# Two hybrid layers on one core: S5 by blocks of four tokens, its rotations and scan on VectorE

## The chip, the cores and the metric

The kernel runs on 1 core of one Trainium2 chip. The metric is device time in microseconds (us) of one launch; 3 runs of the kernel before are at hand, and one execution of it was taken by the hardware profiler. All rows below come from that execution. Engines are PE (TensorE matmul), DVE (VectorE), ACT (ScalarE), POOL (GpSimd) and SP (SyncE, which issues most DMAs).

## What is computed

256 tokens of width 2048 pass through two layers. In each, a norm and one product with `w_in` feed three mixers side by side: NSA (sparse attention, 8 heads), S5 (a diagonal complex state space, width 512) and GDN (gated delta rule, 8 heads of 128). Their outputs go through `w_out` into the residual; an FFN of inner width 5504 with a convolution over three tokens follows. The mixer that the change touches is, cut to what matters:

```python
def s5_mixer(u, lam_re, lam_im, log_dt, b_re, b_im, c_re, c_im, d_skip, w_glu):
    ug = u.reshape(B_, L, 32, 16)                    # 32 groups of 16 channels
    dt = exp(log_dt); mag = exp(lam_re * dt)         # 64 states in a group
    lb_re, lb_im = mag * cos(lam_im * dt), mag * sin(lam_im * dt)
    bb = coef(lb, lam) * (b_re + i b_im)             # complex, [g, p, h]
    bu = einsum('blgh,gph->blgp', ug, bb)            # complex
    x_t = lb * x_(t-1) + bu_t                        # over all 256 tokens
    y = einsum('blgp,ghp->blgh', xr, c_re) - einsum('blgp,ghp->blgh', xi, c_im)
    y = gelu(y + d_skip * ug);  return y * sigmoid(y @ w_glu)
```

Two groups of 16 channels share one tile of 128 states: a *pair*. There are 16 pairs, four of them to each of the four tiles `ct` of 128 channels.

## The kernel before

**Weights.** All large products have the tokens along 256 columns. Weights come from DRAM in tiles of 128x1024 (`raw`, three buffers, issued on SP's queue at L336). ACT rounds each to its high part `whi`, DVE subtracts to get the low part `wlo` (L325 and L326, three buffers each), and every product is three single-pass matmuls: xh·whi, xl·whi, xh·wlo, into the PSUM tile `gps`. A tile of 1024 columns so gives 24 matmuls of 256 columns. `z`, GDN's gate, is computed with tokens on partitions and 512 columns (`gps<-wlo,xh`).

**Order.** `PLANS` gives the emission order of a layer: `xs` (small columns), `u0` to `u3` (S5's input), `tab` (S5's tables), then between `S(` and `S)` the heads `h0` to `h6` of GDN with its solves `g` and gates `z`, while `tick()` hands out S5's queued steps between them; then NSA and the out-projection's passes. The FFN follows in two halves of its 43 tiles f. The scheduler of the framework places the instructions on the engines' queues from there; each engine works its own queue in order.

**GDN head.** `gdn_head` (L1184) squares and sums q and k, takes a power of their norms on POOL (`gsk`, L1213), scales `vt` to `vb` on ACT and builds two triangular matrices, which `gdn_solve` inverts with round trips through DRAM (`scr`, L1258).

**S5.** `s5_tables` (L956) computes in float the coefficients (DVE, 16 columns), the input matrices (six POOL products at L1008 to L1013, eight transposes on PE at L1018, split, written to `parts` in DRAM), and e^{i theta t} for t < 128 as the table `tb`, by doubling (L1043 to L1050, on POOL). Layer 0 runs it after `u0`, layer 1 between the halves of the FFN of layer 0. Then each pair (`s5_pair`, L1070) reads `ub` from `parts` (L1078), makes two matmuls of 256 columns, rotates by `tb` from PSUM (L1087, L1088, DVE), adds and subtracts on POOL (L1089, L1090), scans the decay over 4 pieces of 128 (L1097, DVE, two pieces for the real and two for the imaginary part, with a small turn by `pend` between, L1102, L1103), rotates back on POOL (L1107 to L1110), and `s5_out` (L1113) multiplies by C: eight matmuls per tile that each fill 32 of 128 rows (`mpsm<-tX,cm`). POOL makes what `either()` (L494) doesn't give to DVE; here numbers 0 and 4 alone go to DVE, so all of S5's numbers, 8 to 14, go to POOL.

## Time and profile before

| what | value |
|---|---|
| three runs, us | 2607.79, 2611.43 (median), 2614.37 |
| span of the profiled execution, us | 2613.3 |
| PE, DVE, ACT, POOL busy | 96%, 72%, 46%, 19% |
| mean granted TensorE clock | 0.978 |
| read from HBM over the span | 172 GB/s |

No time is given for the profiled execution apart from its span, first to last instruction, so 2613.3 is taken as its own time; it lies between the runs. Busy time is the sum of an engine's instruction records; matmuls are pipelined, so PE's records overlap one another, and a share near 100% says only that PE is seldom empty. A clock of 1.00 is 2.4 GHz. The stages by time are: to 334 us S5 and GDN of layer 0 (from 28 us on), to 548 NSA and out-projection, to 1328 the FFN (with the tables of layer 1 at 830 to 877), to 1377 the start of layer 1, to 1631 its S5 and GDN, to 1882 its NSA and out-projection, to 2610 its FFN.

### The profile page before, as it was taken

What the parts mean: (1) busy time and instruction counts of PE and PEld (TensorE: products, weight loads), DVE (VectorE), ACT (ScalarE), POOL (GpSimd) and SP (SyncE); (2) the same over time, 40 slices, a digit from 0 to 9 for tenths busy, and PEclk for the clock granted to TensorE, in tenths of its full rate; (3) what the DMA queues carried; (4) which work ended last, traced back from release to release, by engine and by line L of the source; (5) the groups of instructions that cost most, each with busy time, mean ns of one, the idle gap of its engine ahead of it and who ended that gap; (6) DMA issues with size and microseconds to landing.
All of it is one profiled execution on the core that took longest, in us unless ns stands there. A gap on an engine that the chain in (4) does not pass through costs nothing.

```text
span 2613.3 us, 51295 instructions
## 1 busy us (share of the span) xinstructions
PE 2519.4 (96%) x20686; PEld 2426.6 (93%) x20686; DVE 1884.8 (72%) x3252; ACT 1203.4 (46%) x1883; POOL 493.1 (19%) x530
## 2 busy tenths in 40 slices
...
GB/s 276 178 166 124 124 184 155 95 210 169 180 184 197 182 186 183 182 185 190 199 210 176 164 133 120 215 128 99 188 180 185 185 179 181 189 182 182 184 192 166
DMA packets 170974, 456.72 MB, mean 175 GB/s; under 512 B 25040, under 2 KB 55152, under 8 KB 170736
## 3 DMA queue, kind: packets, MB, share of 16 engines
...
q0 software_dynamic: 512, 0.98, 0.1%
...
HBM read 434.81 MB, written 15.48 MB: 172 GB/s over the span
## 4 chain that ended last, share of the span: by engine, by line
PE 74%; DVE 13%; POOL 5%; DMA 4%; issue 3%; ACT 1%; SPq 0%; DVEq 0%; ACTq 0%; POOLq 0%
PE gps L293 69%; DVE wlo L326 4%; DVE tW L1097 2%; DVE cva L441 2%; PE mpsh L293 2%; PE mpss L293 2%; PE mpsm L293 1%; DMA raw<-w 1%; POOL bt L1255 1%; POOL tX L1107 1%; POOL ub L1257 1%; ACT whi L325 1%; POOL s5tmp L1108 1%; POOL s5tmp L1089 1%; DMA ks<-ks 1%
## 5 line engine op out<-in xcount | busy, mean ns | idle before, releaser
L325 ACT ACTIVATE whi<-raw 128x1024 fp32r<-128x1024 f32 (+5 forms) x824 | 824.8, 1002 | 1070.9 <-PE gps L293 717.8
L326 DVE TENSOR_TENSOR wlo<-raw,whi 128x1024 fp32r<-128x1024 f32 (+5 forms) x824 | 985.0, 1196 | 454.2 <-ACT whi L325 450.8
L293 PE MATMUL gps<-xh,wlo 128*128 128x256 f32 x3904 | 1121.4, 287 | 15.7 <-DVE wlo L326 15.6
L293 PE MATMUL gps<-xh,whi 128*128 128x256 f32 x3904 | 1120.1, 287 | 8.9 <-DVE cvp L434 6.2
L293 PE MATMUL gps<-xl,whi 128*128 128x256 f32 x3904 | 1118.1, 287 | 0.0
L293 PEld LDWEIGHTS gps<-xh,wlo 128*128 128x128 f32 x3904 | 759.9, 195 | 22.4 <-DVE wlo L326 18.0
L293 PEld LDWEIGHTS gps<-xh,whi 128*128 128x128 f32 x3904 | 760.2, 195 | 15.4 <-DVE cvp L434 7.2
L293 PEld LDWEIGHTS gps<-xl,whi 128*128 128x128 f32 x3904 | 760.0, 195 | 2.0 <-issue 1.4
L293 PE MATMUL gps<-gh,wlo 128*128 128x256 f32 x1376 | 390.2, 284 | 4.5 <-DVE wlo L326 4.4
L293 PE MATMUL gps<-gl,whi 128*128 128x256 f32 x1376 | 389.9, 283 | 0.0
L293 PE MATMUL gps<-gh,whi 128*128 128x256 f32 x1376 | 389.5, 283 | 0.0
L293 PEld LDWEIGHTS gps<-gh,wlo 128*128 128x128 f32 x1376 | 264.4, 192 | 5.3 <-DVE wlo L326 5.3
L293 PEld LDWEIGHTS gps<-gl,whi 128*128 128x128 f32 x1376 | 264.4, 192 | 0.0
L293 PEld LDWEIGHTS gps<-gh,whi 128*128 128x128 f32 x1376 | 264.2, 192 | 0.0
L434 DVE TENSOR_TENSOR cvp<-gps,R 128x256 f32<-128x256 f32 x220 | 92.6, 422 | 83.4 <-PE gps L293 83.4
L293 PE MATMUL gps<-mh,wlo 128*128 128x256 f32 x512 | 150.4, 297 | 1.0 <-DVE wlo L326 1.0
L293 PE MATMUL gps<-mh,whi 128*128 128x256 f32 x512 | 150.4, 296 | 0.8 <-ACT whi L325 0.7
L293 PE MATMUL gps<-ml,whi 128*128 128x256 f32 x512 | 150.7, 296 | 0.0
L293 PEld LDWEIGHTS gps<-mh,wlo 128*128 128x128 f32 x512 | 102.4, 201 | 2.4 <-DVE wlo L326 1.2
L293 PEld LDWEIGHTS gps<-mh,whi 128*128 128x128 f32 x512 | 102.2, 201 | 1.4 <-ACT whi L325 1.2
L293 PEld LDWEIGHTS gps<-ml,whi 128*128 128x128 f32 x512 | 102.5, 201 | 0.6 <-issue 0.4
L441 DVE SCALAR_TENSOR_TENSOR cva<-cvp,parm,cva 128x255 f32<-128x255 f32 x144 | 95.6, 664 | 0.9
...
## 6 DMA issues: line engine op xcount, KB each, us to landing
...
raw<-w SPq DMA_DIRECT2D x192, 448.0 KB
...
```

Of the source, the lines that this page charges most:

```text
L293: self.nc.tensor.matmul(out, lhsT, rhs, start=start, stop=stop)
L325: self.nc.scalar.activation(out=hi, in_=src, func=AF.Copy)
L326: (engine or self.nc.vector).tensor_tensor(lo, src, hi.bitcast(F32), OP.subtract)
L434: nc.vector.tensor_tensor(p, ps, R, OP.mult)
L441: nc.vector.scalar_tensor_tensor(a[:, j:], p[:, :T - j], tap(n - 1 - j), a[:, j:], OP.mult, OP.add)
L1089: self.either(10).tensor_tensor(A[:, 0:256], A[:, 0:256], B[:, 256:512], OP.add)
L1097: nc.vector.tensor_tensor_scan(W[:, o:o + SCAN], mg, A[:, o:o + SCAN], ini[j], OP.mult, OP.add)
L1107: nc.gpsimd.tensor_tensor(v(X), v(W), cb, OP.mult)
L1108: nc.gpsimd.tensor_tensor(v(B), v(W), sb, OP.mult)
L1255: be.tensor_tensor(t[:, 0:n, 0:m], ub[:, 0:n, j:j + 1].to_broadcast([4 * nb, n, m]), bk[:, j:j + 1, n:].to_broadcast([4 * nb, n, m]), OP.mult)
L1257: be.tensor_tensor(ub[:, 0:n, n:], ub[:, 0:n, n:], t[:, 0:n, 0:m], OP.subtract)
```

## The change

A block of four tokens is one step. The input of a step is now the four tokens' channels along 128 partitions (`U`, read back from `us` in DRAM, four reads of 32 partitions per tile), so per pair one full-precision matmul of 64 columns for each of the real and imaginary parts. One scan of 512 elements covers four pairs, two parts and 64 steps (the decay `m4` is set to 0 at the start of each 64). Both rotations and their sums go to DVE. The output of token j in a block takes three products per pair: from the block's own inputs (a triangular matrix of 96 rows), from the real and from the imaginary state before it.

These need new matrices per layer: for each `ct` `s5_blocks` multiplies the input coefficients and C by powers of lambda (by recurrence, `times`), transposes two of the results, multiplies C and B for the triangular one, and writes 640 columns per pair to `parts`. The emission order gets `t0` to `t3` among the `u`s of layer 0; for layer 1 the blocks come in the second half of the FFN of layer 0, ahead of f = 24, 28, 32 and 36. The table `tb` ends at 64 columns. `either(12)` is POOL. The old functions stand above; of the diff, new functions and the call sites:

```diff
-     ("xs u0 tab u1 u2 u3 S( h0 h1 h2 z0 h3 g0 h4 g2 h5 z1 h6 S) N( kc vc q0 ks g4 h7 cmp q1 kw q2 key P5 "
+     ("xs u0 tab u1 t0 u2 t1 u3 t2 t3 S( h0 h1 h2 z0 h3 g0 h4 g2 h5 z1 h6 S) N( kc vc q0 ks g4 h7 cmp q1 kw q2 key P5 "
       "P0 q3 res att g6 p0 a0 a1 o0 p1 N) o1 p2 o2",
       ((13, 11, 8, 4, 5, 12, 6), (10, 15, 14, 9), (7, 0, 1, 2, 3)), 0.8869, (0, 4)),
...
-SCAN = 128
-NS = T // SCAN
+SUB = 4
+TABLES = (24, 28, 32, 36)
+NC4 = T // SUB
...
                 for f in fs:
+                    if hf and not last and f in TABLES:
+                        self.l += 1
+                        self.s5_blocks(TABLES.index(f))
+                        self.l -= 1
...
                 elif k < 8:
-                    self.split_to(mh[k], ml[k], self.so[:, k - 4, :])
+                    blk = lambda v: v.rearrange("p (c r) -> p c r", r=SUB)
+                    self.split_to(blk(mh[k]), blk(ml[k]), self.so[:, k - 4, :].rearrange("p (r c) -> p c r", r=SUB))
...
                 u = self.uT[int(d)]
-                nc.vector.tensor_tensor(u, ps, self.R, OP.mult)
-                hl = [self.slot("uh", F32R), self.slot("ul", F32R)]
-                self.split_to(*hl, u)
-                for i in range(2):
-                    nc.sync.dma_start(self.parts[self.l][i::2, int(d), :, 0:256].rearrange("r c t -> c r t"),
-                                      hl[i].bitcast(F32).rearrange("p (o t) -> p o t", o=1).to_broadcast([128, 2, T]))
+                blk = lambda v: v.rearrange("p (c r) -> p c r", r=SUB)
+                nc.vector.tensor_tensor(u.rearrange("p (r c) -> p c r", r=SUB), blk(ps), blk(self.R), OP.mult)
+                nc.sync.dma_start(self.us[self.l][int(d)], u)
...
+            elif a == "t":
+                if self.l == 0:
+                    self.s5_blocks(int(d))
...
+        self.lam, self.coef = [], []
+        for to, by, nm in ((self.lam, (br, bi), "l"), (self.coef, (cr, ci), "c")):
+            for i, v in enumerate(by):
+                w = s5.tile([128, 16, 2], F32, name=f"s5{nm}{i}")
+                nc.vector.tensor_copy(w, v.rearrange("p (q o) -> p q o", o=1).to_broadcast([128, 16, 2]))
...
+        self.m4 = st("m4")
+        tt(self.m4, mag, mag, OP.mult)
+        tt(self.m4, self.m4, self.m4, OP.mult)
+        pc, pq = square(*square(cs, sn))
+        self.tb = tb = s5.tile([128, 2, 16, NC4], F32, name="tb")
+        self.s5v = self.pool("s5v", 1, "right")
...
+        gt = self.either(12).tensor_tensor
+        while n < NC4:
...
+    def s5_blocks(self, ct):
+
+        nc, s5 = self.nc, self.s5v[1]
+        gt = self.either(12).tensor_tensor
+        src = self.ap[f"s5m{self.l}"].rearrange("p m (t q h) -> p m t q h", t=4, q=4)[:, :, ct]
+
+        V = s5.tile([128, 4 * 512], F32, name="s5V", tag="s5V")
+        v6 = V.rearrange("p (q r b s h) -> p q r b s h", q=4, r=2, b=2, s=4)
+        at = lambda m: bass.AP(tensor=V.tensor, offset=V.offset + 32 * (3 - m),
+                               ap=[V.ap[0], [256, 8], [128 + 32 * (2 * m - 3), 2], [1, 32]])
+        sb = s5.tile([128, 4, 2, 32], F32, name="s5b", tag="s5b")
+        for r in range(2):
+            nc.scalar.dma_start(sb[:, :, r, :], src[:, r])
+            nc.scalar.dma_start(v6[:, :, r, 1, 0, :], src[:, 2 + r])
+
+        def times(out, x, by, n):
+
+            shape = [128, 8, n, 32]
+            t = [self.s5t()[:, 0:256 * n].rearrange("p (a b h) -> p a b h", a=8, b=n) for _ in range(2)]
+            for i in range(2):
+                w = by[i][:, 4 * ct:4 * ct + 4].rearrange("p q (r a b) -> p (q r) a b", a=1, b=1)
+                gt(t[i], x, w.to_broadcast(shape), OP.mult)
+            gt(out[:, 0::2], t[0][:, 0::2], t[1][:, 1::2], OP.subtract)
+            gt(out[:, 1::2], t[0][:, 1::2], t[1][:, 0::2], OP.add)
+
+        times(at(0)[:, :, 0:1], sb.rearrange("p q (r a) h -> p (q r) a h", a=1), self.coef, 1)
+        nb = s5.tile([128, 4, 32], F32, name="s5n", tag="s5n")
+        self.either(12).tensor_scalar(nb, v6[:, :, 1, 0, 3, :], -1.0, None, OP.mult)
+        for m in range(3):
+            times(at(m + 1), at(m), self.lam, 2)
+
+        d = self.parts[self.l][4 * ct:4 * ct + 4]
...
+        for r in range(2):
+            nc.sync.dma_start(rows(384 + 128 * r, 128), v6[:, :, r, 1].rearrange("p q s h -> p q (s h)"))
+            pt = self.mps("s")
+            for q in range(4):
+                nc.tensor.transpose(pt[:, 128 * q:128 * q + 128], v6[:, q, r, 0].rearrange("p s h -> p (s h)"),
+                                    self.c("ident"))
+            g = s5.tile([128, 512], F32, name="s5g", tag="s5g")
+            nc.scalar.activation(out=g, in_=pt, func=AF.Copy)
+            nc.sync.dma_start(rows(128 * r, 128), g.rearrange("p (q s) -> p q s", q=4))
+
+        W = s5.tile([128, 4, 4, 32], F32, name="s5W", tag="s5W")
+        self.either(12).memset(W, 0.0)
+        pt = self.mps("s")
+        p4 = pt.rearrange("p (q j h) -> p q j h", q=4, j=4)
+        for q in range(4):
+            for r in range(2):
+                for i in range(3):
+                    self.mm(p4[32 * i:32 * i + 32, q, i + 1:4, :].rearrange("p j h -> p (j h)"),
+                            nb[:, q, :] if r else v6[:, q, 0, 0, 3, :],
+                            v6[:, q, r, 1, 0:3 - i, :].rearrange("p j h -> p (j h)"), start=(r == 0), stop=(r == 1))
+        for i in range(3):
+            o = slice(32 * i, 32 * i + 32)
+            nc.scalar.activation(out=W[o, :, i + 1:4, :], in_=p4[o, :, i + 1:4, :], func=AF.Copy)
+        nc.sync.dma_start(rows(256, 128), W.rearrange("p q j h -> p q (j h)"))
+        if ct == 3:
+            self.close(self.s5v[0])
...
+        st = {}
+        self.later(lambda: self.s5_in(ct, st), lambda: self.s5_scan(ct, st), lambda: self.s5_out(ct, st))
+
+    def s5_in(self, ct, st):
+        nc, s5 = self.nc, self.s5
+        U = s5.tile([128, 4, NC4 + 2], F32, name="s5U", tag="s5U", bufs=2)
+        ends = bass.AP(tensor=U.tensor, offset=U.offset, ap=[U.ap[0], [NC4 + 2, 4], [NC4, 2]])
+        nc.gpsimd.memset(ends, 0.0)
+        d = self.us[self.l]
+        for i in range(4):
+            o = 0 if i == 3 else 1
+            nc.sync.dma_start(U[32 * i:32 * i + 32, :, o:o + NC4],
+                              d[ct, :, NC4 * ((i + 1) % 4):NC4 * ((i + 1) % 4) + NC4].rearrange("(q h) c -> h q c", q=4))
+        st["U"], st["g"] = U, []
+        bu = self.mps()
         for q in range(4):
-            self.later(lambda q=q: xs.__setitem__(q, self.s5_pair(ct, q)))
-        self.later(lambda: self.s5_out(ct, xs))
-
-    def s5_pair(self, ct, q):
+            g = s5.tile([128, 256], F32, name="s5gi", tag="s5gi", bufs=4)
+            nc.sync.dma_start(g, self.parts[self.l][4 * ct + q, :, 0:256])
+            for r in range(2):
+                o = 128 * q + 64 * r
+                self.mm(bu[:, o:o + 64], g[:, 128 * r:128 * r + 128], U[:, q, 0:NC4])
+        sh = [128, 4, 2, NC4]
+        v = lambda t: t.rearrange("p (q r c) -> p q r c", q=4, r=2)
+        tb = lambda i: self.tb[:, i, 4 * ct:4 * ct + 4].rearrange("p q (r c) -> p q r c", r=1).to_broadcast(sh)
+        A, B = self.s5t(), self.s5t()
+        tt = nc.vector.tensor_tensor
+        tt(v(A), v(bu), tb(0), OP.mult)
+        tt(v(B), v(bu), tb(1), OP.mult)
+        tt(v(A)[:, :, 0], v(A)[:, :, 0], v(B)[:, :, 1], OP.add)
+        tt(v(A)[:, :, 1], v(A)[:, :, 1], v(B)[:, :, 0], OP.subtract)
+        m = s5.tile([128, 512], F32, name="s5m", tag="s5m", bufs=2)
+        m4 = self.m4[:, 4 * ct:4 * ct + 4].rearrange("p (q r c) -> p q r c", r=1, c=1)
+        nc.gpsimd.tensor_copy(v(m), m4.to_broadcast(sh))
+        nc.gpsimd.memset(v(m)[:, :, :, 0:1], 0.0)
+        st["A"], st["m"], st["tb"], st["v"] = A, m, tb, v
+        for q in range(4):
+            g = s5.tile([128, 384], F32, name="s5go", tag="s5go", bufs=5)
+            nc.sync.dma_start(g, self.parts[self.l][4 * ct + q, :, 256:640])
+            st["g"].append(g)
+
+    def s5_scan(self, ct, st):
         nc, s5 = self.nc, self.s5
-        sh = [128, 2, NS, SCAN]
...
+        tt, v, tb = nc.vector.tensor_tensor, st["v"], st["tb"]
...
+        nc.vector.tensor_tensor_scan(W, st["m"], st["A"], 0.0, OP.mult, OP.add)
+        X = s5.tile([128, 512], F32, name="tX", tag="tX", bufs=4)
         B = self.s5t()
...
+        tt(v(X), v(W), tb(0), OP.mult)
+        tt(v(B), v(W), tb(1), OP.mult)
+        tt(v(X)[:, :, 0], v(X)[:, :, 0], v(B)[:, :, 1], OP.subtract)
+
+        nc.vector.scalar_tensor_tensor(v(X)[:, :, 1], v(X)[:, :, 1], -1.0, v(B)[:, :, 0], OP.mult, OP.subtract)
+        st["X"] = X
...
+        U, X, g = st["U"], st["v"](st["X"]), st["g"]
+        for j in range(SUB):
+            for i in range(3):
+                for q in range(4):
+                    w = g[q][:, 128 * i + 32 * j:128 * i + 32 * j + 32]
+                    self.mm(yp[32 * q:32 * q + 32, 64 * j:64 * j + 64], w[0:96] if i == 0 else w,
+                            U[0:96, q, 1:NC4 + 1] if i == 0 else X[:, q, i - 1], start=(i == 0), stop=(i == 2))
```

`order` of the instructions on an engine's queue follows at three places, engine, line, operation, and what is written and read. On POOL, layer 0, around the power `gsk` of the second head, L1213 before and L1270 after. Before, tables (L1045, L1050), then pairs:

```order
L1213 TENSOR_TENSOR gsk<-gS,cst 128x2
L1045 TENSOR_TENSOR tb<-tb,s5tmp 128x8x64
L1050 TENSOR_TENSOR tb<-tb,s5tmp 128x8x64
L1089 TENSOR_TENSOR s5tmp<-s5tmp 128x256
L1090 TENSOR_TENSOR s5tmp<-s5tmp 128x256
L1107 TENSOR_TENSOR tX<-tW,tb 128x512
L1108 TENSOR_TENSOR s5tmp<-tW,tb 128x512
L1089 TENSOR_TENSOR s5tmp<-s5tmp 128x256
L1090 TENSOR_TENSOR s5tmp<-s5tmp 128x256
L1109 TENSOR_TENSOR tX<-tX,s5tmp 128x256
L1110 TENSOR_TENSOR tX<-tX,s5tmp 128x256
```

and after, where `times` is L1073 to L1075, `s5l` are the powers' lambda and `s5c` the input's coefficients:

```order
L1073 TENSOR_TENSOR s5tmp<-s5V,s5l_529 128x512
L1073 TENSOR_TENSOR s5tmp<-s5V,s5l_531 128x512
L1074 TENSOR_TENSOR s5V<-s5tmp 128x4x2x32
L1075 TENSOR_TENSOR s5V<-s5tmp 128x4x2x32
L1073 TENSOR_TENSOR s5tmp<-s5V,s5l_529 128x512
L1073 TENSOR_TENSOR s5tmp<-s5V,s5l_531 128x512
L1073 TENSOR_TENSOR s5tmp<-s5b,s5c_533 128x256
L1073 TENSOR_TENSOR s5tmp<-s5b,s5c_535 128x256
L1270 TENSOR_TENSOR gsk<-gS,cst 128x2
L1074 TENSOR_TENSOR s5V<-s5tmp 128x4x2x32
L1075 TENSOR_TENSOR s5V<-s5tmp 128x4x2x32
```

The power stood between parts of two S5 pairs; it now stands between the products of the second block and those of the third (the 256-column products start a block).

On SP, layer 0, at the first reads of S5's inputs. Before, with `ub` as the input of a pair:

```order
L336 DMA raw<-w 128x1024
L1023 DMA parts_88<-s5tmp 128x4x128 x2
L336 DMA raw<-w 128x1024 x2
L1078 DMA ub<-parts_88 128x1x512 x2
L336 DMA raw<-w 128x1024
L1078 DMA ub<-parts_88 128x1x512
L336 DMA raw<-w 128x1024 x2
L1078 DMA ub<-parts_88 128x1x512
L336 DMA raw<-w 128x1024 x2
```

and after, where `s5gi` and `s5go` are the matrices of one pair for input and output, and `s5U` the inputs of a tile:

```order
L337 DMA raw<-w 128x1024
L1093 DMA parts_90<-s5g 128x4x128
L1108 DMA parts_90<-s5W 128x4x128
L1130 DMA s5gi<-parts_90 128x256
L1124 DMA s5U<-us_88 32x4x64 x4
L1130 DMA s5gi<-parts_90 128x256 x3
L1150 DMA s5go<-parts_90 128x384 x4
L1124 DMA s5U<-us_88 32x4x64 x4
L1130 DMA s5gi<-parts_90 128x256 x4
L1150 DMA s5go<-parts_90 128x384
L1303 DMA scr_86<-nq 128x2x128
L337 DMA raw<-w 128x1024 x2
```

Before, loads of weights (`raw`) stood between the single reads; now the reads of the first two tiles stand in a row behind the fourth block's writes (L1093, L1108).

On PE, layer 0, at the first input products of S5. Before, behind the products of k and q of GDN's first head:

```order
L293 MATMUL gps<-xl,whi 128x256
L293 MATMUL mpsh<-gk 128x256
L293 MATMUL mpsh<-gk 128x128
L293 MATMUL mpsh<-gq,gk 128x256
L293 MATMUL mpsh<-gq,gk 128x128
L293 MATMUL mpsm<-ub 128x256 x2
L293 MATMUL gps<-xh,wlo 128x256
```

and after, where `mpss<-gU,gP` is GDN's solve of the first two heads:

```order
L294 MATMUL gps<-xh,wlo 128x256
L294 MATMUL mpss<-gU,gP 32x32 x3
L294 MATMUL mpsm<-s5U,s5gi 128x64 x2
L1282 MATMUL mpsh<-cst,vt 128x128
L294 MATMUL mpsm<-s5U,s5gi 128x64 x4
L1282 MATMUL mpsh<-cst,vt 128x128
L294 MATMUL mpss<-gU,gP 32x32 x2
L294 MATMUL mpsm<-s5U,s5gi 128x64 x2
L294 MATMUL mpss<-gU,gP 32x32 x11
```

The first input products moved from the first head's products to the first solve, from behind 455 `gps` products to behind 1017 (counted from the start of the program).

## Rows read from the trace of the kernel before

**Rows 1.** The page: busy time, share of the span and instructions of each engine.

```profile
PE 2519.4 (96%) x20686; PEld 2426.6 (93%) x20686; DVE 1884.8 (72%) x3252; ACT 1203.4 (46%) x1883; POOL 493.1 (19%) x530
```

**Rows 2.** Windows: stretch, busy us (instructions) of PE, PEld, DVE, ACT, POOL; clock, DMA.

```profile
28.00:334.00 306.00, 272.30 (x2132) 244.22 (x2132) 279.90 (x561) 118.50 (x202) 199.28 (x194) 0.94 0.51 160
830.00:877.00 47.00, 42.54 (x349) 41.73 (x348) 38.99 (x52) 16.73 (x18) 41.03 (x46) 1.00 0.65 195
1377.00:1631.00 254.00, 229.57 (x1856) 207.39 (x1855) 237.47 (x449) 101.47 (x179) 142.86 (x137) 0.95 0.45 144
1882.00:2610.00 728.00, 727.51 (x6048) 727.31 (x6048) 464.47 (x636) 336.16 (x432) 0.00 (x0) 1.00 0.56 182
```

**Rows 3.** Groups on PE, 1377 to 1631 us: busy us, mean ns | idle before.

```profile
L293 PE MATMUL gps<-xh,wlo 128*128 128x256 f32 x321 | 95.9, 299 | 5.2 <-DVE wlo L326 5.2
...
L293 PE MATMUL gps<-wlo,xh 128*128 128x512 f32 x64 | 25.6, 400 | 1.4 <-DVE wlo L326 1.3
...
L293 PE MATMUL mpsh<-cst,gsq 128*128 128x1 f32 x56 | 7.9, 259 | 4.1 <-ACT gsq L1205 4.1
...
L293 PE MATMUL mpsm<-tX,cm 128*32 128x256 f32 x64 | 6.6, 390 | 1.2 <-POOL tX L1109 1.0 <-POOL tX L1110 0.2
...
L293 PE MATMUL mpss<-gU,gP 64*64 64x64 f32 x16 | 1.3, 224 | 0.0
```

**Rows 4.** Timeline of PE from 138 us: start, duration.

```profile
138.91 0.40 PE L293 MATMUL gps<-wlo,xh 128*128 128x512 f32 x1
139.14 0.40 PE L293 MATMUL gps<-whi,xl 128*128 128x512 f32 x1
```

**Rows 5.** Groups on DVE, 1377 to 1631 us.

```profile
L326 DVE TENSOR_TENSOR wlo<-raw,whi 128x1024 fp32r<-128x1024 f32 x58 | 81.0, 1396 | 4.8 <-ACT whi L325 4.7
L1097 DVE TENSOR_TENSOR_SCAN tW<-s5mag,s5tmp 128x128 f32<-128x128 f32 x32 | 21.1, 673 | 7.0 <-POOL s5tmp L1089 7.0
...
L1097 DVE TENSOR_TENSOR_SCAN tW<-s5mag,s5d,s5tmp 128x128 f32<-128x128 f32 x32 | 13.6, 466 | 0.1
...
L1087 DVE TENSOR_TENSOR s5tmp<-mpsm,tb 128x512 f32<-128x512 f32 x16 | 10.8, 677 | 0.3 <-PE mpsm L293 0.3
...
L434 DVE TENSOR_TENSOR cvp<-gps,R 128x256 f32<-128x256 f32 x20 | 8.2, 409 | 0.1
L1195 DVE TENSOR_TENSOR_SCAN E<-eb,cst 128x256 f32<-128x256 f32 x7 | 5.9, 838 | 0.0
...
L1103 DVE TENSOR_TENSOR s5d<-s5e 128x2 f32<-128x2 f32 x16 | 2.5, 157 | 0.1
```

**Rows 6.** Groups on DVE, 1900 to 2100 us, in the FFN of layer 1.

```profile
L326 DVE TENSOR_TENSOR wlo<-raw,whi 128x1024 fp32r<-128x1024 f32 x70 | 85.8, 1226 | 38.1 <-ACT whi L325 38.1
L434 DVE TENSOR_TENSOR cvp<-gps,R 128x256 f32<-128x256 f32 x35 | 14.9, 425 | 17.3 <-PE gps L293 17.3
```

**Rows 7.** Groups on POOL, 1377 to 1631 us.

```profile
L1108 POOL TENSOR_TENSOR s5tmp<-tW,tb 128x512 f32<-128x512 f32 x16 | 31.2, 1951 | 0.0
...
L1109 POOL TENSOR_TENSOR tX<-tX,s5tmp 128x256 f32<-128x256 f32 x16 | 13.4, 836 | 0.7
```

**Rows 8.** Groups on PE, 28 to 334 us.

```profile
L1018 PE MATMUL mpsm<-cst,s5tmp 128*128 128x128 f32 x8 | 1.2, 276 | 0.1
```

**Rows 9.** Groups on POOL, 830 to 877 us.

```profile
L1045 POOL TENSOR_TENSOR tb<-tb,s5tmp 128x512 f32<-128x512 f32 x3 | 5.8, 1927 | 0.0
...
L1043 POOL TENSOR_TENSOR tb<-tb,s5pc 128x512 f32<-128x512 f32 x3 | 3.1, 1048 | 0.0
```

**Rows 10.** Timeline of POOL: start, duration.

```profile
46.37 1.05 POOL L1009 TENSOR_TENSOR s5tmp<-s5tmp,s5ci 128x512 f32<-128x512 f32 x1 [1.73 <-DVE s5t L1052]
...
122.26 1.02 POOL L1213 TENSOR_TENSOR gsk<-gS,cst 128x2 f32<-128x2 f32 x1 [0.80 <-DVE fe L1212]
```

**Rows 11.** Instructions of tile `ub`: ns (min, median, max), first and last start.

```profile
L1078 SPq DMA_DIRECT2D ub<-parts x32: 524/535/743, 73.5 to 1559.9; - x32
```

**Rows 12.** Groups on DVE, 830 to 877 us.

```profile
L326 DVE TENSOR_TENSOR wlo<-raw,whi 128x1024 fp32r<-128x1024 f32 x6 | 9.7, 1623 | 2.3 <-ACT whi L325 2.3
```

128 lines of the change are left out of this document (27 added, 101 removed), and 2 rows, old and new, of the table PLANS.

## Prediction, made before the changed kernel was run

> **What bounds the kernel now.** I read the page first: TensorE (PE) is busy 96% of the span and VectorE (DVE) 72% [rows 1]. Pipelined matmuls overlap, so a busy PE says little. The pace says more: in the FFN of layer 1 PE issues 6048 matmuls in 728 us, one in 0.120 us, and DVE has a third of its time free [rows 2]. That is PE's own pace, and the FFN stages, more than half of the span, stand at it. The reader should see where this is not so: the two stretches in which S5 runs beside the GDN heads, 28 to 334 us in layer 0 and 1377 to 1631 us in layer 1. There DVE is busy 280 of 306 and 237 of 254 us, GpSimd (POOL) 199 and 143 us [rows 2].
>
> What PE would need in the second stretch: 962 matmuls of 256 columns (three groups of 320 or 321 [rows 3]) at 0.120 are 116 us. The 192 of 512 columns follow each other at 0.23 us [rows 4], 44 us. The 18 other groups, from the squares' sums to the 64x64 products, are busy 75 us together [rows 3]. Their records too are longer than their distance (0.30 against 0.12 us, 0.40 against 0.23), so I take two thirds, 50 us. Sum 210 of 254: **44 us are lost**. Layer 0's stretch holds 276 records more [rows 2], 33 us: 243 of 306, **63 us lost**. By row, PE's visible waits there are for the weights' low parts on DVE [rows 3], and DVE's longest wait that is not for weights is its scan waiting for a POOL sum [rows 5]. So here DVE, and POOL through it, set the pace.
>
> **What goes from these stretches.** Per layer 16 pairs of groups become 4 tiles, each with instructions of the same size as one pair had. On DVE go, in layer 1, the scans (21.1 and 13.6 us), the two rotations from PSUM (10.8 each, one shown) and two small products per pair (2.5 each, one shown): 61 us [rows 5]. On POOL go six groups between 31.2 and 13.4 us [rows 7]; all six make 122 us. Each new tile has on DVE two PSUM rotations at 0.68 [rows 5], four sums of 256 columns at 0.43 like cvp [rows 6], two rotations of 512 columns from SBUF at about 0.65 (half a wlo of 1024 at 1.23 [rows 6]) and one scan of 512. The scans shown take 0.47 for 128 and 0.84 for 256 columns [rows 5], so 512 should take 1.6. Together 5.9, four tiles 24 us.
>
> DVE is also slower beside POOL: wlo takes 1.396 us in this stretch [rows 5] and 1.226 in the FFN [rows 6], 10 us over 58 of them. The convolution's taps and the solves give about as much. So DVE falls from 237 to about 180 us against PE's 210. That is a fuller DVE than in the FFN, but no longer the bound.
>
> **What PE gets.** Before, a tile cost 8 single-pass records (1 us by the pace) and eight output products that run four side by side, 64 records in 6.6 us a layer [rows 3], 1.6 a tile. Now the input products are 8 in full precision, two records each. A transposing record of that kind takes 0.15 (8 in 1.2 us [rows 8]), so 2.4 a tile. The output is 48 products of 64 columns in 12 groups of four; by the four-abreast row (0.8 a group at 256 columns) a group takes 0.2 to 0.3, 3 us. Net 2.8 a tile, 11 us a layer. Below, if none of it adds to the chain, nothing; above, if the four do not overlap, 48 x 2 x 0.15 = 14 a tile, 45 us a layer more. I take 11, because the shown row has them overlap.
>
> Each block of the new matrices (four a layer) has 8 transposes, 16 records or 2.4 us, and 24 small products whose 48 records lie between 1.3 (abreast) and 7 (one after another): 4 us a block taken, **16 a layer**, bounds 15 and 38.
>
> **What POOL gets.** A block is on POOL six products of 512 columns (an instruction of that size takes 1.05 to 1.93 [rows 9]), six sums of 256 (0.84 [rows 7], in a bad case half as much again) and, as an estimate from these, 3 us of small ones: 14 to 22 us. Four blocks: 55 to 88. Against this the doubling of the tables stops at 64 columns, which saves the 12 long instructions of the last level, some 18 us of the 41 that POOL is busy between 830 and 877 us [rows 2], and the old input matrices' six products.
>
> **Layer 0.** Here the blocks lie in the same stretch as S5. By the order, POOL works at them without a pause until the fourth, and only then can the first S5 tile read its matrices: its products on PE stand behind 1017 weight products where the first pair stood behind 455. POOL can start at about 48 us, since its products with S5's coefficients ran from 46 [rows 10]. Tables take 20 us (half of the 41), then come four blocks at 16 and three waits for the one V buffer, which I guess at 4 each: 144 us. The fourth block's transposes stand behind 950 weight products, 854 of the 1440 in the old stretch: by even pace PE was there at 28 + 306 x 854/1440 = 209 us. Even 50 us earlier it comes after POOL. The pow of head 1 (gsk) ran on POOL at 122 us [rows 10]; now it stands behind two blocks, at about 48 + 20 + 32 + 4 = 104, so it is not late. What is queued behind it if it were: ACT's vb, and on ACT's queue the next weights' high parts. SP issues some 22 reads in a row before the next weight load; at 0.54 like the old ones [rows 11] that is 12 us, against three raw buffers and three split ones ahead, each 24 matmuls or 2.9 us, 17 us in all. This costs 0 to 5. Lost 63, minus 16 + 11 of new work and minus what the first 120 us still lose to POOL: at most 36 to gain, and I take **22**.
>
> **Layer 1.** No block is in the stretch, and POOL is left with some 27 us. 44 lost, 11 of new work: at most 33. FFN-like stretches lose little, but the GDN solves' round trips stay, so I take **24**.
>
> **FFN of layer 0.** PE is the bound, so the 16 us of blocks come on top in full. Between 830 and 877 us the old tables beside POOL made 349 matmuls take 47 us instead of 42 [rows 2]: 5 lost in 41 us of POOL. Now POOL has some 23 + 70 us there: 11, so 6 more. If POOL never disturbs, 0; if twice as much, 17 more. Waits of a block for its neighbour are covered: the blocks are four of the FFN's f apart, 384 matmuls or 46 us. Cost **22**.
>
> A rule weighed here. Where POOL is always busy, a wlo of 1024 columns takes 1.62 [rows 12] instead of 1.23, while cvp, with one operand in PSUM, keeps its 0.41 beside POOL [rows 5] and 0.43 without [rows 6]. The Trainium skill ("SBUF — State Buffer", section "Who interferes with whom") says why: a VectorE instruction with two SBUF inputs and a GpSimd instruction that reads SBUF lock each other out for a whole instruction, and one with a single SBUF input is free. The trace agrees for these two rows. Taken at its worst, the rule makes each wlo wait for a whole POOL product; what that would give is among the rivals.
>
> **Sum.** 2613.3 (span of the profiled execution, inside the runs' 2607.79 to 2614.37) - 22 - 24 + 22 = 2589; the median of the runs is 2 lower, so **2587**. About 0.3%, 8 us, is what a measurement of this kernel tells from no change.
>
> **Rivals.**
> - Forecast, faster by 10 to 45: chance 0.53.
> - Nearly all that is lost comes back (36 and 33) and the blocks cost PE 15 with no disturbance: 2613 - 69 + 15 = 2559, minus 2: 2557. For it: with 180 of 210 DVE is hardly fuller than where the FFN runs at pace. Against it: round trips of the solves. Chance 0.15.
> - The lost time is the GDN chain's, not DVE's: DRAM round trips and solves stay where they are, gains fall to 10 and 12, 2613 - 22 + 22 = 2613, no change. For it: PE's records also wait for squares on ACT and taps on DVE, each a step of a chain. Chance 0.10.
> - POOL holds up every DVE instruction for a whole one of its own. In the FFN DVE is 64% busy [rows 2]; if each wlo waited for a product of 1.6 us it would cost 2.8, DVE would need 1.4 of its time over the 93 us of POOL, and PE lose 30 of them where 11 are in the sum; with the same in layer 0's first 120 us some 5 more: 2587 + 24 = 2611, no change. The 1.62 under a full POOL speaks against it. Chance 0.05.
> - Slower: POOL becomes the wait in layer 0. If a block takes 22 us and the waits for V 6, the fourth ends at 48 + 20 + 88 + 18 = 174, and PE, which has no S5 to do before that, may stand at its transposes from 155 on: 19 us on top of the sum. If disturbance in the FFN is twice what I take, that costs 11 more: the span's sum minus 2 is then 2587 + 19 + 11 = 2617. It decides from about 17 us a block, (155 - 48 - 20 - 18) / 4. For it: POOL's 1.93 beside DVE [rows 9]; against: the 1.05 at 46 us [rows 10], with DVE as full. Chance 0.17.
>
> So faster 0.68, same 0.15, slower 0.17. The range leaves out the tails: 2553 (both losses regained) to 2619 (half of the slower case); the likeliest case alone spans 2566 to 2603.
>
> **What would show it.** In the changed profile DVE should be near 180 us in layer 1's S5 stretch, with wlo near 1.25 there; that stretch should last about 230 us. Scans: eight of about 1.6 us. A block's transposes in the FFN should not wait for POOL, and the FFN of layer 0 should be some 22 us longer. Wrong would be: PE waiting at the fourth block in layer 0, ACT's vb waiting for gsk, SP's weight loads held by a parts write, or s5go products that follow at 0.15 instead of four abreast.

## The result: 2533 us against 2610, and the profile after

| | before | after | ratio, 95% interval |
|---|---|---|---|
| median, us | 2609.61 (2602.77 to 2614.37) | 2533.03 (2529.15 to 2541.02) | 0.9721 [0.9695, 0.9746] |
| span of the profiled execution | 2613.3 | 2539.1 | |

The change makes the kernel 77 us faster, where 24 were forecast and the range ended at 2553. To see where, both traces are cut at the same weight products (the starts of the 1681st, 9281st, 10537th and 11961st `gps<-` matmul), so that each stretch holds the same ones. The third column is an experiment, told below: the change with one small tile 64 bytes wider.

| stretch, us by the trace | before | after | a_pad64 |
|---|---|---|---|
| S5 and GDN of layer 0 | 360.1 | 341.3 | 343.6 |
| NSA, out-projection and FFN of layer 0 | 999.8 | 1000.5 | 1010.2 |
| start of layer 1, its S5 and GDN | 274.2 | 233.5 | 237.7 |
| NSA and out-projection of layer 1 | 252.8 | 251.4 | 251.0 |
| FFN of layer 1, tail | 726.4 | 712.5 | 726.2 |

The page of the kernel after, busy time, share and instructions, to be set beside [rows 1]:

```profile
PE 2487.4 (98%) x21822; PEld 2408.8 (95%) x21822; DVE 1774.0 (70%) x3058; ACT 1220.9 (48%) x1911; POOL 362.7 (14%) x470
```

Windows of the kernel after, columns as in [rows 2]: the two S5 stretches, then 100 us each of the FFN of layer 1, in the products with the input and in those with the gated inner values:

```profile
28.00:315.00 287.00, 267.82 (x2621) 249.03 (x2620) 222.82 (x452) 125.21 (x218) 132.63 (x163) 0.96 0.61 180
1354.00:1575.00 221.00, 221.00 (x2220) 205.79 (x2219) 170.42 (x357) 102.83 (x183) 28.48 (x48) 1.00 0.54 169
1900.00:2000.00 100.00, 100.00 (x836) 100.00 (x835) 72.62 (x106) 50.28 (x70) 0.00 (x0) 1.00 0.56 184
2080.00:2180.00 100.00, 100.00 (x884) 100.00 (x884) 51.30 (x55) 39.97 (x41) 0.00 (x0) 1.00 0.63 195
...
2430.00:2530.00 100.00, 100.00 (x885) 100.00 (x884) 52.10 (x57) 40.26 (x43) 0.00 (x0) 1.00 0.72 207
```

Two things are to be seen. Layer 1's S5 stretch is full: PE has records in all of its 221 us, where [rows 2] has 229.57 of 254, and DVE is busy 170. Its granted clock rose with that from 0.95 to 1.00. And the FFN, whose code the change doesn't touch, has a second pace: 884 matmuls in 100 us where [rows 2] has 6048 in 728, or 831. It shows only where the moving tile is `gh` or `gl`. The granted clock is 1.00 at both paces, the 2.4 GHz level.

Groups on DVE in the kernel after, 1354 to 1575 us, to be set beside [rows 5]:

```profile
L327 DVE TENSOR_TENSOR wlo<-raw,whi 128x1024 fp32r<-128x1024 f32 x59 | 71.9, 1218 | 17.5 <-ACT whi L326 17.3
...
L1157 DVE TENSOR_TENSOR_SCAN tW<-s5m,s5tmp 128x512 f32<-128x512 f32 x4 | 4.8, 1212 | 0.0
...
L1161 DVE TENSOR_TENSOR s5tmp<-tW,tb 128x512 f32<-128x512 f32 x4 | 3.6, 891 | 0.0
```

Groups on PE there, S5's input products and the two kinds of output products:

```profile
L294 PE MATMUL mpsm<-s5U,s5gi 128*128 128x64 f32 x64 | 7.8, 272 | 0.0
...
L294 PE MATMUL mpsm<-tX,s5go 128*32 128x64 f32 x256 | 7.0, 220 | 0.0
L294 PE MATMUL mpsm<-s5U,s5go 96*32 96x64 f32 x128 | 6.1, 224 | 0.0
```

### The profile page after: what moved, and what is told of

It is laid out like the page before. It is cut to its first block, busy times and chain, and to the rows that moved or that the text cites. A ratio compares the mean times of both kernels' runs of the same rounds, so it can differ in the third digit from the quotient of the medians.

```text
span 2539.1 us, 53497 instructions
## 1 busy us (share of the span) xinstructions
PE 2487.4 (98%) x21822; PEld 2408.8 (95%) x21822; DVE 1774.0 (70%) x3058; ACT 1220.9 (48%) x1911; POOL 362.7 (14%) x470
## 4 chain that ended last, share of the span: by engine, by line
PE 88%; DVE 4%; POOL 3%; DMA 2%; issue 1%; ACT 1%; SPq 0%; ACTq 0%; DVEq 0%; POOLq 0%
PE gps L294 78%; PE mpss L294 3%; PE mpsh L294 3%; PE mpsm L294 2%; DVE wlo L327 1%; POOL s5tmp L1073 1%; DMA parts<-s5g 1%; ACT whi L326 1%; DMA raw<-w 1%; PE mpss L905 0%; DVE cva L442 0%; POOL s5tmp L1043 0%; POOL s5tmp L1046 0%; POOL s5V L1074 0%; POOL s5V L1075 0%
## 5 line engine op out<-in xcount | busy, mean ns | idle before, releaser
L327 DVE TENSOR_TENSOR wlo<-raw,whi 128x1024 fp32r<-128x1024 f32 (+5 forms) x824 | 971.0, 1179 | 476.4 <-ACT whi L326 473.3
L294 PEld LDWEIGHTS gps<-xh,whi 128*128 128x128 f32 x3904 | 752.6, 193 | 9.9 <-ACT whi L326 4.4
L294 PE MATMUL gps<-gl,whi 128*128 128x256 f32 x1376 | 379.6, 276 | 0.0
L294 PE MATMUL gps<-gh,wlo 128*128 128x256 f32 x1376 | 379.6, 276 | 0.0
L294 PE MATMUL gps<-gh,whi 128*128 128x256 f32 x1376 | 379.2, 276 | 0.0
L442 DVE SCALAR_TENSOR_TENSOR cvag<-cvp,parf,cvag 128x255 f32<-128x255 f32 (+1 forms) x172 | 89.5, 521 | 5.1 <-ACT cvag L440 2.2
```

Source lines behind the costliest of these rows:

```text
L294: self.nc.tensor.matmul(out, lhsT, rhs, start=start, stop=stop)
L327: (engine or self.nc.vector).tensor_tensor(lo, src, hi.bitcast(F32), OP.subtract)
L442: nc.vector.scalar_tensor_tensor(a[:, j:], p[:, :T - j], tap(n - 1 - j), a[:, j:], OP.mult, OP.add)
```

## Experiments: the pace of the FFN

Theory: PE's time for a weight product depends on the byte at which the moving tile lies, and the change moved tiles. (The moving tile is the operand whose 256 columns pass through PE, such as `xh` or `gh`; `whi` and `wlo` are the weights that it meets there.) It dropped small tiles (`s5pend`, `s5e`, `s5d`) and added `s5m4`, so by the program's allocation all that lies behind the small tiles went down by 320 bytes a partition: `gh` and `gl` from 0 past a multiple of 256 bytes to 192. The weights and the tiles of the FFN's input stayed at 0. Rival: the FFN is faster through something that the change does, such as S5's idle POOL.

**a_pad64 and b_pad64** put 64 bytes behind the same small tile in the kernel after and in the one before. `gh` and `gl` then lie at 0 and at 64. The instructions and their order are unchanged.

```diff
-        t2 = st("t2")
+        t2 = self.sm.tile([128, 32], F32, name="s5t2", tag="s5t2", bufs=1)[:, 0:16]
```

> The changed kernel with one small tile widened by 64 bytes, which puts gh and gl back on multiples of 128 bytes; nothing else differs. Theory A: output matmuls of the FFN back at 0.120, 27.5 us longer than the changed kernel, 2533 + 27.5 = 2560, ratio to before about 0.981; this is then what the change is worth by its S5 part alone. Theory B: as the changed kernel, 2533, ratio 0.972.

> The kernel before with one small tile of S5 widened by 64 bytes, and nothing else: every instruction stands where it stood, but all tiles that lie behind the small ones (those of GDN, and the FFN's gated products gh and gl among them) move by 64 bytes, as they did by another 320 in the change. Theory A (PE's pace hangs on where its moving tile starts: 0.1133 us a matmul of 256 columns at 64 past a multiple of 128 bytes, 0.120 at a multiple): the FFN's 4128 output matmuls gain 6.7 ns each, 27.5 us in all, ratio to before about 0.9895, with FFN input matmuls still at 0.120. Theory B (the faster output matmuls come from what the change does to the other engines or the queues, not from addresses): ratio 1.000, all at 0.120.

Windows of a_pad64, input and output products of the FFN of layer 1:

```profile
1900.00:2000.00 100.00, 100.00 (x835) 100.00 (x834) 71.70 (x105) 50.98 (x70) 0.00 (x0) 1.00 0.55 184
2100.00:2200.00 100.00, 100.00 (x836) 100.00 (x835) 48.45 (x51) 37.12 (x38) 0.00 (x0) 1.00 0.60 185
```

The same of b_pad64, output products:

```profile
2125.00:2225.00 100.00, 100.00 (x851) 100.00 (x851) 49.25 (x52) 38.04 (x39) 0.00 (x0) 1.00 0.60 187
```

a_pad64 took 2561.29 us, 0.9819 [0.9796, 0.9843]: 28 us of the change's 77 go with the place of these tiles, and by the profiles the output products alone take 27.4 us longer. b_pad64 took 2603.42, 0.9976 [0.9960, 0.9993], with a third pace between the others, where 0.1133 was expected. A record lasts 0.28 us, so a window counts some two more than begin in it; by starts the paces are 0.1200, 0.1178 and 0.1133 us.

**b_gh192** puts `gh` and `gl` of the kernel before at 192, by 96 bytes in each of the two buffers of the tile ahead of them; the order stays the same.

```diff
-g = fp.tile([128, T], F32, name="gg", tag="gg")
+g = fp.tile([128, T + 24], F32, name="gg", tag="gg")[:, 0:T]
```

> The kernel before with one tile of the FFN (gg) 96 bytes wider in each of its two buffers, so that gh and gl start at 192 past a multiple of 256 bytes, as in the changed kernel; with the earlier run they started at 64 and the output matmuls took 0.1178 us. All instructions stand where they stood. Theory A2 (the place within 256 bytes sets the pace: 0.120 at 0 and 128, 0.1178 at 64, 0.1133 at 192): output matmuls at 0.1133, 27.5 us less than before, ratio 0.9895. Theory B2 (the place only opens the way, and what else the changed kernel does decides between 0.1178 and 0.1133): as the earlier run, 0.1178, ratio 0.9965 to 0.998.

Windows of b_gh192, output products of layer 0, first half, and of layer 1:

```profile
880.00:940.00 60.00, 60.00 (x511) 60.00 (x511) 29.63 (x32) 22.75 (x23) 0.00 (x0) 1.00 0.60 189
...
2100.00:2200.00 100.00, 100.00 (x883) 100.00 (x882) 53.13 (x59) 40.70 (x43) 0.00 (x0) 1.00 0.61 191
```

It took 2583.45 us, 0.9890 [0.9863, 0.9917]: 27 us, by the interval 22 to 36, without any part of the change. The theory holds and the rival falls. The two layers have 4128 of these products; at 0.1200 - 0.1133 that is 27.7 us. In this profile they took 20.8 us less, since the first of the FFN's four halves gave only 0.4: it began at 0.1133, but at 838 us, beside the tables on POOL, PE stood for 2.9 us, its clock fell (a mean of 0.92 from 836 to 880 us), and it came out of that at 0.1178 (511 records in 60 us above).

**a_slots64 and a_slots192** move the other moving tiles too (`xh`, `xl`, `mh`, `ml`, all in 48 slots) by an empty tile of 64 or 192 bytes ahead of the slots. With a_pad64's edit beside it, `gh` and `gl` then lie at 64 or 192 as well. **a_table**, a single run, lengthens `gh`, `gl`, `whi` and `wlo` by 32 bytes and starts every other `gh` and `gl` 16 bytes later: these two come to eight places within 128 bytes, the three buffers of `whi` to 0, 32 and 64 and those of `wlo` to 96, 128 and 160. `xh` and `xl` lie at 192 there.

```diff
+            pd.tile([128, 48], F32, name="pad")
```

> The changed kernel with an empty tile of 64 bytes ahead of the 48 slots, in which xh, xl, mh and ml lie, and a small tile widened by 64 so that what lies behind keeps its place within 128 bytes. Theory A: the FFN's 8256 input matmuls at 0.1133 too, 55 us less, and of the 4,100 or so others with 256 columns between nothing and all, up to 27 more: 2450 to 2478, ratio 0.939 to 0.950. Theory B: 2533, ratio 0.971. Theory C (what counts is the distance of the moving tile from the weights, not its own address) gives the same as A here, since the weights stay where they are.

> The changed kernel with 192 empty bytes ahead of the slots and 64 more behind, so that xh, xl, mh and ml as well as gh and gl start at 192 past a multiple of 256 bytes. Theory A2: all FFN matmuls at 0.1133; 8256 input matmuls by 6.7 ns are 55 us less than the changed kernel, with up to 27 from the mixers' products: 2450 to 2478, ratio 0.939 to 0.950. Theory B2: a mix of 0.1133 and 0.1178 as with the slots at 64, about 2523, ratio 0.967.

> The changed kernel with gh and gl 32 bytes longer and every other one started 16 bytes later, so that they start at eight places within 128 bytes, and with the split weights 32 bytes longer, so that whi starts at 0, 32 and 64 and wlo at 96, 0 and 32 within 128; the slots land at 64. One profile gives the pace for every pair of places. Theory A: the pace hangs on the moving tile alone: 0.1133 at 64 and 0.120 at 0 whatever the weights; of the other places nothing is known. Theory C: by the distance: with weights at 64, a moving tile at 64 is slow (0.120) and one at 0 fast (0.1133).

Windows of a_slots64: FFN outputs of layer 0, first and second half, and FFN inputs of layer 1:

```profile
850.00:950.00 100.00, 100.00 (x852) 100.00 (x851) 52.38 (x58) 40.11 (x43) 0.00 (x0) 1.00 0.62 188
1200.00:1270.00 70.00, 70.00 (x620) 70.00 (x619) 43.25 (x59) 35.59 (x50) 0.00 (x0) 1.00 0.74 211
1900.00:2000.00 100.00, 100.00 (x851) 100.00 (x850) 73.40 (x107) 51.23 (x70) 0.00 (x0) 1.00 0.59 188
```

Windows of a_slots192, FFN inputs of layer 0 and of layer 1:

```profile
650.00:750.00 100.00, 100.00 (x885) 100.00 (x884) 76.46 (x111) 54.00 (x74) 0.00 (x0) 1.00 0.65 195
1900.00:2000.00 100.00, 100.00 (x852) 100.00 (x850) 73.33 (x107) 50.99 (x70) 0.00 (x0) 1.00 0.57 186
```

They took 2523.25 us, 0.9673 [0.9657, 0.9689], and 2502.36, 0.9540 [0.9475, 0.9604], the latter with a wide spread, 2473.53 to 2513.89 (the profile is of the last). The place alone was expected to give 2450 to 2478. Both faster paces appear at the same addresses: 620 in 70 us is 0.113, 851 in 100 is 0.1178. PE keeps the pace that it has until something disturbs it: a_slots64 went from 0.1178 to 0.1133 behind layer 0's blocks in the FFN, a_slots192 from 0.1133 to 0.1178 there, and each stayed so to the end of the layer. a_table took 2534.47; all eight places of `gh` and `gl` gave gaps between 0.112 and 0.125, with means of 0.117 to 0.119. Its input products had their moving tiles at 192 as in a_slots192, and of what they read only the weights lay elsewhere: in layer 1 they took 0.1183, 0.1176 and 0.1199 on the mean by which of the three weight buffers they used. So the weights' place takes part, and the moving tile's place does not set the pace by itself. What PE does inside is open.

## Experiments: S5's part

By a_pad64 against before, S5's change alone is worth 45 us in the profiles (2613.3 - 2568.6) and 48 in the medians, where 24 were forecast. Two theories: it is the move off POOL, or it is the blocks of four with their 4 chains of instructions a layer in place of 16.

**b_dve** makes only the move, in the kernel before: all of S5's sums and rotations on DVE. **a_pool** takes it back in the kernel after, for five of the eight instructions of a tile (of the other three, two were on DVE before). The cut shows b_dve.

```diff
-PLANS ... 0.8869, (0, 4)
+PLANS ... 0.8869, (0, 4, 8, 9, 10, 11)
...
-nc.gpsimd.tensor_tensor(v(X), v(W), cb, OP.mult)
-nc.gpsimd.tensor_tensor(v(B), v(W), sb, OP.mult)
+nc.vector.tensor_tensor(v(X), v(W), cb, OP.mult)
+nc.vector.tensor_tensor(v(B), v(W), sb, OP.mult)
```

> The kernel before with S5's sums and rotations, six POOL instructions a pair, on VectorE: the move of the change without its blocks. By the rows of before DVE gets 16 x (4 x 0.42 + 2 x 0.68) = 49 us more a layer in a stretch of 254 in which it is busy 237, and is quicker elsewhere by about 25 for want of POOL beside it. Theory D (the fewer instructions of the blocks paid, not the move): 0 to 20 us slower, ratio 1.000 to 1.008. Theory E (the move paid): 20 us faster or more, ratio 0.992 or below.

> The changed kernel with S5's rotations back on POOL as before: the two sums of the first rotation, the two products of the second and one of its sums (five of eight instructions a tile). It undoes the move to VectorE and keeps the blocks of four tokens. Theory D (what paid in the two S5 stretches is that each tile costs a quarter of the instructions, on whichever engine): DVE gets 4 x 3 = 12 us a layer less and POOL 4 x 8 = 32 us more, and with DVE at 170 of 221 us in layer 1 and POOL at 28 nothing waits: within 8 us of the changed kernel, 2533, ratio 0.968 to 0.974. Theory E (what paid is that POOL no longer disturbs DVE and stands in no tile's chain): a third to a half of the 53 us gained by the S5 part comes back, 2550 to 2560.

Windows of layer 1's S5 stretch in b_dve:

```profile
1364.00:1603.00 239.00, 221.31 (x1724) 197.32 (x1723) 224.16 (x531) 98.28 (x171) 28.38 (x40) 0.95 0.47 151
```

and in a_pool:

```profile
1354.00:1580.00 226.00, 223.67 (x2217) 206.72 (x2217) 170.96 (x334) 103.27 (x183) 49.92 (x68) 0.99 0.51 163
```

Groups on DVE in b_dve, 1364 to 1603 us, the stretch of [rows 5]:

```profile
L326 DVE TENSOR_TENSOR wlo<-raw,whi 128x1024 fp32r<-128x1024 f32 x58 | 70.5, 1215 | 10.8 <-ACT whi L325 10.7
...
L1097 DVE TENSOR_TENSOR_SCAN tW<-s5mag,s5tmp 128x128 f32<-128x128 f32 x32 | 12.0, 403 | 0.0
L1107 DVE TENSOR_TENSOR tX<-tW,tb 128x512 f32<-128x512 f32 x16 | 11.0, 687 | 0.0
L1108 DVE TENSOR_TENSOR s5tmp<-tW,tb 128x512 f32<-128x512 f32 x16 | 11.0, 685 | 0.0
```

b_dve took 2590.01 us, 0.9922 [0.9908, 0.9936], 20 us faster; a_pool 2538.47, 0.9713 [0.9687, 0.9740], the same as the change. So the move alone gives 20 of 48, and the blocks give all of it, within the noise, without most of the move. In layer 1 the same products take 257 us before, 240 with the move (b_dve), 226 with the blocks (a_pool) and 221 with both. The two gains do not add, so both cure in part the same loss; the rows point to POOL's long instructions in each pair's chain and beside DVE. An L1108 takes 0.69 us on DVE where it took 1.95 on POOL [rows 7], and the wait of 7.0 us for POOL's sums [rows 5] is gone from the scan. With POOL busy 28 us instead of 143, wlo falls from 1.396 [rows 5] to 1.215: 10 us that DVE gets back. The Trainium skill ("SBUF — State Buffer", section "Who interferes with whom") has GpSimd and two-input VectorE instructions on SBUF shut each other out; the trace agrees, 1.215 with little of POOL, 1.396 with more of it, 1.62 under a full one [rows 12].

**a_noblk** leaves layer 1's blocks out of the FFN of layer 0; layer 1 then reads layer 0's matrices, so it does the same work on other numbers. **a_blkdve** has tables and blocks on DVE.

```diff
-                        self.l += 1
-                        self.s5_blocks(TABLES.index(f))
-                        self.l -= 1
...
-PLANS ... 0.8869, (0, 4)
+PLANS ... 0.8869, (0, 4, 12)
```

> The changed kernel without the four blocks of layer 1 that stand in the FFN of layer 0; layer 1 reads the matrices of layer 0, so its S5 output is not that of the reference. It measures what the blocks cost in a stage that PE bounds. Theory F (a block costs PE its own matmuls and no more: 2.5 us each by the lengthening of 384 matmuls around one, and one block's start at 600 us beside the tables): 10 to 13 us less than the changed kernel, 2521. Theory G (the blocks' POOL work slows the weights' splits on DVE by more than shows at the blocks): 20 us or more less, 2513 or below.

> The changed kernel with the tables' doubling and the blocks' products and sums on VectorE in place of POOL. In layer 0 POOL ended the fourth block at 180 us, with waits of 10 to 13 us for the one V buffer between blocks, and PE lost 13 us there against before. Theory J (POOL's slower instructions make that loss): on DVE a block takes about 8 us instead of 16, S5 starts earlier in layer 0, 5 to 10 us less in all, 2525, ratio 0.967. Theory K (the waits between the blocks' stages on PE, DMA and POOL make it, not the engine; and each instruction on DVE now stands ahead of a weight tile's split): same or slower by up to 10, 2533 to 2543, ratio 0.970 to 0.974.

a_noblk took 2518.16 us, 0.9639 [0.9609, 0.9669]: 15 less than the change by medians. In its profile (of the run of 2509.76) layer 0's NSA, out-projection and FFN take 977.0 us, 23.5 less. Some 2.5 us lie at each block; another 9 lie around the first, where 1000 weight products (the 3200th to the 4200th) take 130.0 us in the change and 120.7 here.

a_blkdve took 2526.97 us, 0.9675 [0.9657, 0.9693], 6 less than the change by medians. By profiles layer 0's S5 stretch has 329.2 us instead of 341.3. What that stretch loses in the change is in the timeline of POOL of the kernel after: each block waits for the transposes of the one before to free the V buffer, then for the new one's loads:

```profile
95.39 0.46 POOL L1074 TENSOR_TENSOR s5V<-s5tmp 128x128 f32<-128x128 f32 x1 [5.16 <-PE mpss L294]
...
101.42 2.94 POOL L1073 TENSOR_TENSOR s5tmp<-s5V,s5l 128x512 f32<-128x512 f32 x2 [4.34 <-DMA s5V<-s5m]
...
157.88 0.46 POOL L1074 TENSOR_TENSOR s5V<-s5tmp 128x128 f32<-128x128 f32 x1 [8.92 <-PE mpss L294]
...
163.61 2.50 POOL L1073 TENSOR_TENSOR s5tmp<-s5V,s5l 128x512 f32<-128x512 f32 x2 [4.24 <-DMA s5V<-s5m]
...
180.20 0.10 POOL L1120 MEMSET s5U<- 128x8 f32 x1
```

and the waits of PE there, 60 to 300 us (total, times, longest):

```profile
PE mpss L1089 <- POOL s5V L1074: 7.7, 3, 3.9
PE gps L294 <- DVE wlo L327: 6.6, 5, 1.8
```

On DVE the blocks' products of 512 columns take half, as the group in a_blkdve's trace (28 to 300 us) shows; in the change they take 1.38 us on POOL:

```profile
L1073 DVE TENSOR_TENSOR s5tmp<-s5V,s5l 128x512 f32<-128x512 f32 x24 | 15.4, 680 | 2.8 <-DMA s5V<-s5m 2.8
```

## Experiments: the queues that feed the weights

The 9 us at the first block: SP's queue shows it, in the kernel after. The write of V (L1086) stands between the weight loads, and it waits for POOL:

```profile
600.83 28.35 SPq L337 DMA_DIRECT2D raw<-w  x9
633.64 1.06 SPq L1086 DMA_DIRECT2D parts<-s5V  x2
635.81 24.13 SPq L337 DMA_DIRECT2D raw<-w  x10
```

ACT's queue has the block's reads, in the same way. In the kernel after, 603 to 660 us, ACT waits with a weight tile:

```profile
ACT whi L326 <- POOL s5tmp L1073: 5.4, 1, 5.4
```

**a_q** puts the reads of layer 1's blocks on POOL's queue, **a_wq** the writes of V, in both layers, there and the other writes on ACT's, **a_qwq** does both.

```diff
-            nc.scalar.dma_start(sb[:, :, r, :], src[:, r])
+            (nc.gpsimd if self.l else nc.scalar).dma_start(sb[:, :, r, :], src[:, r])
...
-            nc.sync.dma_start(rows(384 + 128 * r, 128), v6
+            nc.gpsimd.dma_start(rows(384 + 128 * r, 128), v6
```

> The changed kernel with the reads of the blocks' B and C in the FFN of layer 0 issued from POOL's own queue in place of ACT's; in layer 0's mixers they stay on ACT's. In the changed kernel's trace ACT stands 5.4 us with a weight tile's high part at about 630 us behind such a read, which waits until POOL has used the buffer; PE then lacks weights, and that stretch of 1000 products takes 130 us where it took 120 without the blocks. Theory H (the queue is the cause): 8 to 10 us less than the changed kernel, 2524, ratio 0.967, and the four later blocks still 2.5 us each. Theory I (POOL's tables and block beside DVE's splits are the cause): no change, 2533, ratio 0.970.

> The changed kernel with the blocks' writes of their matrices taken off SP's queue: those of V go out on POOL's queue, right behind the work that makes them, those of g and W on ACT's, behind the copies that make them. In the run with the reads on POOL's queue SP stood from 625 to 631 us at the first block's write of V, which waits for POOL, with the weight loads behind it, and ACT waited 7.4 us for a weight tile. Theory L (a write that waits on SP for the block holds the weights up): the stretch of 1000 products takes 120 to 122 us where it took 130, and layer 0's stretch before S5's first input gains up to 5 more: 2517 to 2525, ratio 0.964 to 0.967. Theory M (POOL's work beside DVE's splits is the cause): 2533, ratio 0.970.

> The changed kernel with both: in the FFN the blocks' reads on POOL's queue, and all writes of V there too, those of g and W on ACT's behind their copies. Each half alone did not shorten the stretch of 1000 products beside the first block (132 with the reads moved, SP then waiting; 130 with the writes moved, ACT then waiting for the reads). Theory N (either of the two queues that feed the weights, SP or ACT, loses the time as long as one of them holds a transfer that waits for POOL's block): 120 to 123 us now, about 8 less than the changed kernel if the later blocks stay at 2.5 us each; with the reads on POOL's queue two of these took 5 more, so 2525 to 2537 in all. Theory M (POOL's work beside DVE's splits): 130 as before, 2535 to 2545.

Waits of ACT around the first block, in a_q:

```profile
ACT whi L326 <- DMA raw<-w: 7.4, 1, 7.4
```

in a_wq:

```profile
ACT whi L326 <- POOL s5V L1074: 7.1, 1, 7.1
ACT sg L467 <- POOL s5tmp L1073: 6.3, 1, 6.3
```

and in a_qwq:

```profile
ACT whi L326 <- DMA raw<-w: 2.1, 2, 1.3
```

a_q took 2543.76 us, 0.9741 [0.9728, 0.9755], and a_wq 2538.96, 0.9723 [0.9702, 0.9744]: no gain from either, where 8 us or more were expected. With SP's write left in place the next weights come late (7.4); with ACT's reads left in place ACT itself waits for POOL (7.1 and 6.3). With both moved, 2527.38, 0.9684 [0.9664, 0.9704], and the 1000 products take 124.2 us instead of 130.0 (a_q 131.9, a_wq 129.7). So a waiting transfer left on either of the two queues that feed PE costs about the whole stall; with both moved, 6 of the 9 us at this block come back, while the medians of the whole kernel are 6 us apart with intervals that overlap. In a_blkdve, where DVE makes the blocks, the 1000 products take 122.2.

## A version that beats both

To hold 0.1133, **a_relock** versions put the slots at 192, but the first of the 16 row pieces of each input at 0 (two slots of a pool of their own): each pass then comes to 192 from tiles at 0, from where the kernels above had begun at 0.1133 each time. Their other edits are those of the table.

```diff
+    def slot(self, name, dt=F32, k=1):
+        if k == 0:
+            return self.kp0.tile([128, T], dt, name=name, tag="slot0")
...
-mh[k], ml[k] = self.slot("mh", F32R), self.slot("ml", F32R)
+mh[k], ml[k] = self.slot("mh", F32R, k), self.slot("ml", F32R, k)
```

| version, with the edits of | median, us | ratio to before |
|---|---|---|
| a_relock_q: a_q | 2496.24 | 0.9559 [0.9546, 0.9572] |
| a_relock_wq: a_wq | 2487.91 | 0.9522 [0.9494, 0.9550] |
| a_relock_bd: a_blkdve | 2472.37 | 0.9466 [0.9443, 0.9488] |
| a_relock_bdwq: a_blkdve, a_wq | 2466.15 | 0.9447 [0.9427, 0.9466] |
| a_relock_bdqwq: a_blkdve, a_qwq | 2455.91 | 0.9410 [0.9392, 0.9429] |

> As the run before, and with xh, xl, mh and ml at 192 past 256 bytes, except those of the first k-tile, which lie in two slots of their own at a multiple of 256. In the profiles so far a stretch at 192 that is entered from the pace 0.120 (moving tiles at a multiple of 128) locked at 0.1133 first each time, and one disturbed on the way could fall to 0.1178 and stay there. Theory A3 (the pace is locked on entry, and passing through a tile at 0 locks it anew): each product of 16 k-tiles makes three matmuls at 0.120 and the rest at 0.1133, 50 us less over the FFN's 8256 input matmuls and 10 to 20 in the mixers; with the queue 2455 to 2475, ratio 0.941 to 0.949, and little spread between runs. Rival: the level is not set on entry; a mix of 0.1133 and 0.1178 as with all slots at 192, 2465 to 2505.

> As the run before with the slots at 192 past 256 bytes and the first k-tile's in two slots at a multiple of 256, as tried with the reads on POOL's queue: there FFN input matmuls ran at 0.1139 on the mean in both layers. Theories A3 and L together: 2533 - 10 (queue) - 50 (FFN input) - 8 (mixers) = 2465, ratio 0.944. If the two meet the same loss elsewhere, up to 2480.

> The slots placed as in the run before, tables and blocks on VectorE, all writes on SP as in the changed kernel. With the blocks on VectorE alone the kernel took 2527 and its stretch of 1000 products 122 us, since a block is made sooner and SP waits less. Theory A3: 50 us less for the FFN's input, 5 to 10 in the mixers: 2467 to 2475, ratio 0.945 to 0.948.

> All of it: the slots placed, tables and blocks on VectorE, the blocks' writes off SP. If a waiting write on SP is still worth something with the blocks on VectorE, 2 to 6 us less than the run before, 2463 to 2470; if DVE's making of the blocks has taken that away, the same.

> The fastest version so far (slots placed, tables and blocks on VectorE, writes off SP, 2466) with the reads of the FFN's blocks on POOL's queue as well. Theory N: up to 4 us less, 2462 to 2466, since POOL's queue is all but empty here; if the reads come later than from ACT's queue, PE waits for the blocks and it is slower by up to 10.

Windows of a_relock_bdqwq: FFN inputs of layer 0, then inputs and outputs of layer 1:

```profile
650.00:750.00 100.00, 100.00 (x882) 100.00 (x881) 76.00 (x110) 53.26 (x75) 0.00 (x0) 1.00 0.64 194
...
1850.00:1950.00 100.00, 100.00 (x882) 100.00 (x881) 75.56 (x110) 54.01 (x74) 0.00 (x0) 1.00 0.59 195
2000.00:2100.00 100.00, 100.00 (x885) 100.00 (x884) 51.76 (x55) 39.60 (x40) 0.00 (x0) 1.00 0.62 195
```

The last one is 77 us faster than the change. The first two stayed above their expectations, which had counted on a gain from a_q and from a_wq. In all five profiles layer 1's FFN and tail take the same 687.7 us. In the last one's, the first products of a pass, at 0 and just behind, take 0.113 to 0.122 us each and the others there 0.1133. In its profile the FFN of layer 1 takes 684.2 us instead of 709.1, and layer 0's S5 stretch 321.1 instead of 341.3.

## Why the prediction was wrong

**The FFN's pace.** The step that failed: "That is PE's own pace, and the FFN stages, more than half of the span, stand at it." The 0.120 was read rightly, but as a property of PE, while it was one of this layout; the place of the tiles, which the change moves, was costed at nothing by not being named. It gave 28 of the 77 us, more than the forecast's whole gain, and is the reason why the range did not hold the result: without it (a_pad64) 2561 lies inside.

**Layer 1's S5: -24 forecast, -36 measured** (257.2 to 221.0 us in the same products). The mechanism was right: DVE fell to 170.4 us (180 said), wlo to 1.218 (1.25 said), the stretch to 221.0 (230 said). Two terms were off. The new work of PE, "2.8 a tile, 11 us a layer", took too much for what overlaps: the 96 output records of the first tile begin between 1389.84 and 1391.18 us, in 1.34, and 16 input records, 0.111 us apart, take 1.7, so 3.1 a tile against the 2.6 removed, 2 us a layer. And the 9 us kept back for the round trips of the solves were too many: of the 44 lost all came back but some 6. One thing that the prediction did not name helped: [rows 2] has a mean clock of 0.95 over this stretch's 254 us, and the change 1.00. Between the two levels, 2.4 and 1.2 GHz, that is some 25 us at the lower one, so up to 13 of the 36 us came back with the clock, an estimate from these two rows. A scan of 512 took 1.21 us instead of 1.6.

**Layer 0's S5: -22 forecast, -17 measured** (360.1 to 343.6 in a_pad64). The step on POOL was too small: the fourth block ended at 180 us, not 144. POOL's waits ahead of a block for V, its release and its loads, were 9 to 13 us instead of 4, which makes some 21 of these 36; the blocks' own work and the GDN powers between them make the rest. That is the slower rival's mechanism, which put the end at 174. PE was not there at 209 us either, an even pace that the trace of before doesn't bear out: PE had 950 weight products behind it at 182. But PE, which that rival had at the fourth block's transposes from 155 us on, came there at 177.6 and stood 1.9 us; three such waits make 7.7, not 19.

**FFN of layer 0: +22 forecast, +10 measured** (999.8 to 1010.2 in a_pad64). Against a_noblk, corrected by 13.7 us for its faster outputs (977.0 + 13.7 = 990.7), the blocks cost 19.5, where 16 + 11 were in the sum, and 9.1 came back, where 5 were put down for the old tables. The products beside the old tables (the 4913th to the 5968th) give 6.0 of it, 132.7 us against 126.7 in a_pad64; the rest lies in NSA and the out-projection, which took 207.7 us before and 202.0 in b_pad64 with the same instructions, and so is not shown to be the change's. A block takes 2.5 us of PE instead of 4, and most of the disturbance, 6 of the 9 us at the first block, is no slow DVE but the two queues above. "SP's weight loads held by a parts write" stood among the signs of a wrong forecast; at the first block it was so.

**What held.** S5's output products do run four abreast, and the blocks' transposes in the FFN do not wait for POOL. The rival by which DVE is locked out by POOL and the one by which the solves hold the time both fall. The rival "nearly all that is lost comes back", 0.15, came nearest: S5 alone gave 2561, where it said 2557. That is in part luck: of its terms, layer 1 gave 36 where it had 33, but layer 0 gave 17 where it had 36, and the FFN cost 10 where it had 15.
